# Rows of eight tokens for the selected blocks: sixteen gathers in place of thirty-two, in groups tied to neighbouring results, and slabs of x tied in the same way

## The chip, the cores and the metric

One core of a Trainium2 chip runs the whole program, in fp32. The metric is the device time of one execution in microseconds (us); lower is better. TensorE is called PE below, VectorE DVE, ScalarE ACT, GpSimd POOL, and SyncE SP, whose queue issues most of the transfers.

## What is computed

Two layers of a decoder are applied to a prompt of 1024 tokens and to 8 samples of one new token each. Layer 0 has an attention with three branches (compressed, selected blocks, window) beside a convolution module, then an output projection and a feed-forward part. The change touches the selected branch of the samples: each sample and each of its two key/value heads picks 16 of 65 blocks of 64 tokens, and attends to their keys and values, which lie in a paged cache of HBM.

```
def select_blocks(p_cmp, t_pos, ns):
    ...
    score = jnp.where(forced, BIG, jnp.where(valid, score, -BIG))
    _, idx = lax.top_k(score, min(N_SELECT, ns))
    return idx

def nsa_sample(q, kv_c, kv_s, kv_w, gates, ck, li, pool_c, pool_s, win_buf, page_table):
    ...
    idx = select_blocks(p_c, t_pos, ns)
    key_pos = idx[..., None] * SEL_BLOCK + jnp.arange(SEL_BLOCK)
    ...
    phys = page_table[bi, jnp.clip(key_pos // PAGE_SIZE, 0, n_pages - 1)]
    from_pool = pool_s[li, phys, key_pos % PAGE_SIZE, :, gi]
    ...
    o_s = selected_attention(q, t_pos, idx, sel)
```

After the attention `x_prompt` and `x_sample` get the output projection added: `xp = xp + concat([a_out, c_out]) @ w_out_a`. That sum is the x of the slabs below.

## The kernel before

The program is one stream of instructions for each engine. The Tile framework sets the order on each engine with a simulated schedule, so the order follows the order of the Python code, its priorities and the simulated times. The prompt's work is the foreground. The samples' work is a chain of Python generators started with `back=True`; `tick` (L85) advances a planned clock by the foreground's estimated time and takes the next piece of the chain when it is due, at lowered priority (`LAG`). A generator's `yield` is its planned time until the next piece; `WAIT[0]`, 35 us, stands between the issue of the key gathers and the first use of the keys.

The chain runs beside `prompt_attention` (L772) and `out_proj` (L1044) in this order: compressed tokens of the samples' caches (its gathers `pg<-ccmp` at L571), `dec_select` (L829), which ends in the row numbers `vidx` of the selected rows, `dec_gather_k` (L926), `dec_sel_scores` (L945), `dec_gather_v` (L985), `dec_values` (L1003).

**The gathers.** A row of the gathered tables `cslc_k` and `cslc_v` holds four tokens of one head: 256 elements, 1 KB. One sample and head needs 240 rows for its 15 old blocks, in two halves of 128 and 112 partitions. With 16 pairs of sample and head (four tiles of four pairs) that makes 32 indirect DMAs for the keys (L939) and 32 for the values (L996), issued by POOL in its order:

```
for h in range(2):
    m = P - 16 * h
    nc.gpsimd.indirect_dma_start(out=k[:m, n // 2, h, n % 2], out_offset=None, in_=i["cslc_k"],
                                 in_offset=bass.IndirectOffsetOnAxis(
                                     ap=self.vidx[:m, h, 4 * b2 + n:4 * b2 + n + 1], axis=0))
```

`dec_sel_scores` transposes the keys on PE (L955, 64 transposes), copies them to SBUF on ACT (L105, tile `ks`) and multiplies them by the queries (L967). `dec_values` multiplies the weights by the values (L1027).

**The prompt's attention** beside the key gathers: scores (L678, L679), softmax on ACT and DVE, transposes of the weights (L743), copies to `pt` by ACT (L105) and DVE (L117) in turn, products with the values (L762).

**The slabs of x.** `out_proj` splits its inputs z into two parts (`prep`, L1055), loads eight tiles of `w_out` (L123), and for each of eight output tiles m and each chunk of 344 columns runs 24 matmuls (three products for each of eight input tiles, L1112 to L1114) and adds the result to x on DVE (L1080). x lies in four slabs of two output tiles, 1032 KB each. The first is loaded at L1074, the others at L1083, in the code right after an add:

```
a = nc.vector.tensor_tensor(xs, xs, ps, op=ALU.add)
if c == 0 and m % 2 == 0 and m < 6:
    with self.tc.issue_after(a.ins):
        nc.sync.dma_start(x[m // 2 + 1], i["xt"][:, m + 2:m + 4])
```

`issue_after` orders the instruction in the schedule; it puts no wait for the add into the program.

Of the kernel before, what the change touches and what calls it, by code (L numbers as in the profile page):

```python
# [12 lines left out]
I32 = mybir.dt.int32  # L13
# [7 lines left out]
P = 128  # L21
D = 1024
TP = 1024
NS = 8
# [8 lines left out]
KY = 0.8  # L33
LAG = 100
DY = 0.6
TAPLAG = (1000, 2500)
WAIT = (35.0, 5.0)
# [3 lines left out]
class Net:  # L41
# [612 lines left out]
    def att_s1(self, it):  # L654
# [34 lines left out]
        self.att_scale(it, st, br)  # L689

# [111 lines left out]
    def dec_prep(self):  # L802
        nc, i = self.nc, self.i
        nd = i["c_dec"].shape[1]
        dw = self.u([P, 2 * T], name="dw")
        self.dwp = nd

        def d(m, n, dt=F32):
            a = self.dwp
            self.dwp += n  # L810
            t = dw[:m, a:a + n]
            return t if dt == F32 else t.bitcast(dt)
        self.d = d
        cst = self.cst = dw[:, 0:nd]
        nc.sync.dma_start(cst, i["c_dec"])
        self.eb, self.own = cst[:64, 16:24], cst[:64, 358:374]
# [12 lines left out]
    def dec_select(self):  # L829
        nc, d, cst, tb = self.nc, self.d, self.cst, self.tb  # L830
        hsum = cst[:64, 0:16]
        esel, iota62, addv = cst[:16, 24:280], cst[:16, 280:342], cst[:, 342:358]
# [46 lines left out]
        vp = self.ps(self.to(), [P, 2, 16])  # L879
        for h in range(2):  # L880
            nc.tensor.matmul(vp[:, h], esel[:, h * P:(h + 1) * P], pht, start=True, stop=True)
        self.vidx = self.small(P, 32, I32).rearrange("p (a b) -> p a b", a=2)
        nc.vector.scalar_tensor_tensor(self.vidx, vp, 32.0, addv[:, None, :].to_broadcast([P, 2, 16]),
                                       op0=ALU.mult, op1=ALU.add)
        yield DY * 2.0
        self.dec_gather_k()
# [42 lines left out]
    def dec_gather_k(self):  # L929

        nc, i = self.nc, self.i
        self.ksel = []
        self.dw2 = self.u([P, 2 * T], name="dw2")
        for b2 in range(4):
            k = self.u([P, 2, 2, 2, 256], name="ks")
            for n in range(4):
                for h in range(2):
                    m = P - 16 * h
                    nc.gpsimd.indirect_dma_start(out=k[:m, n // 2, h, n % 2], out_offset=None, in_=i["cslc_k"],  # L939
                                                 in_offset=bass.IndirectOffsetOnAxis(  # L940
                                                     ap=self.vidx[:m, h, 4 * b2 + n:4 * b2 + n + 1], axis=0))
            self.ksel.append(k)

    def dec_sel_scores(self):

        nc = self.nc
        yield WAIT[0]
        for b in range(NS):
            k = self.ksel[b // 2][:, b % 2]
            for h in range(2):  # L950
                m = P - 16 * h
                tp = self.ps(self.to(), [P, 512])
                kt = k[:, h].rearrange("p g c -> p (g c)")
                for e in range(4):
                    nc.tensor.transpose(tp[:, e * m:(e + 1) * m], kt[:m, e:512:4], self.ident[:m, :m])  # L955
                self.acopy(kt[:, :4 * m], tp[:, :4 * m])
                if h:
                    nc.vector.tensor_copy(kt[:, 448:449], self.knew[:, 0, b:b + 1])
                yield DY * 0.4
        dw = self.dw2  # L960
        p = dw[:64, 0:961]
        for h in range(2):
            n = 512 - 63 * h
            ps = self.ps(self.to(), [64, 512])
            for b in range(NS):
                kt = self.ksel[b // 2][:, b % 2, h].rearrange("p g c -> p (g c)")
                nc.tensor.matmul(ps[:, :n], self.qz[:, b], kt[:, :n], start=b == 0, stop=b == NS - 1)  # L967
                yield DY * 0.8
            self.acopy(p[:, 512 * h:512 * h + n], ps[:, :n])
# [4 lines left out]
        self.new_key(p, 960, 0)  # L974
        tp = self.ps(self.to(), [P, 4, 2, 64])
        for h in range(2):
            m = P - 16 * h
            for e in range(4):
                nc.tensor.transpose(tp[:m, e, h], p[:, 512 * h + e * m:512 * h + (e + 1) * m], self.ident[:64, :64])
        self.pst = dw[:, 1024:1536].rearrange("p (e h b) -> p e h b", e=4, h=2)  # L980
        self.acopy(self.pst[:, :, 0], tp[:, :, 0])
        self.acopy(self.pst[:112, :, 1], tp[:112, :, 1])
        yield WAIT[1]

    def dec_gather_v(self):  # L985
# [4 lines left out]
        for b2 in range(4):  # L990
            v = self.u([P, 4, 2, 256], name="vsel")
            for e in range(4):
                n = 4 * b2 + e
                for h in range(2):
                    m = P - 16 * h
                    nc.gpsimd.indirect_dma_start(out=v[:m, e, h], out_offset=None, in_=i["cslc_v"],  # L996
                                                 in_offset=bass.IndirectOffsetOnAxis(ap=self.vidx[:m, h, n:n + 1],
                                                                                     axis=0))
# [3 lines left out]
    def dec_values(self):  # L1002
# [3 lines left out]
        for hf in range(2):  # L1006
# [15 lines left out]
            for j in (2 * hf, 2 * hf + 1):  # L1022
                o = ov[:, 256 * (j % 2):256 * (j % 2) + 256].rearrange("p (n d) -> p n d", n=4)
                for h in range(2):
                    m = P - 16 * h
                    for e in range(4):
                        nc.tensor.matmul(o, self.pst[:m, e, h], self.vsel[j][:m, :, h, 64 * e:64 * e + 64],  # L1027
                                         start=False, stop=j % 2 == 1 and h == 1 and e == 3)
                        yield DY * 0.45
# [16 lines left out]
    def out_proj(self):  # L1046
# [21 lines left out]
        def part(chunks):  # L1068
            ws = [self.load_w(i["w_out"][0])]
            for m in range(8):  # L1070
# [4 lines left out]
                for c in chunks:  # L1075
# [396 lines left out]
def dec_consts():  # L1472
    c = np.zeros((P, 374), np.float32)
# [5 lines left out]
    for h in range(2):  # L1479
        c[:16, 24 + h * P:24 + (h + 1) * P] = bg[:, None] == (8 * h + p // 16)[None, :]  # L1480
    c[:16, 280:342] = np.arange(62)
    c[:, 342:358] = (bg % 2)[None, :] * 16 + (p % 16)[:, None]
    c[row, 358 + row // 4] = 1.0
# [3 lines left out]
def arrange(a):  # L1487
# [37 lines left out]
    r["cslc_k"] = cs[:, :, 0].reshape(-1, 16, 4, 2, 64).transpose(0, 3, 1, 4, 2).reshape(-1, 256)  # L1525
    r["cslc_v"] = cs[:, :, 1].transpose(0, 2, 1, 3).reshape(-1, 256)
# [51 lines left out]
```

## Time and profile before

| | |
|---|---|
| median of 3 runs | 2500.28 us (2498.76 to 2510.8) |
| the profiled execution | 2508.53 us |
| its span, first to last instruction | 2506.8 us |
| PE busy in the span | 2380.4 us (95%), 15040 matmuls |
| DVE, ACT, POOL busy | 53%, 30%, 8% |
| granted PE clock, mean of the span | 0.970 |

A span is the time from the first to the last instruction; a share is busy time over the span. In the windows of the section on rows, each engine's busy us stands with its count of instructions in brackets, then the granted PE clock as a fraction of full speed, the busy share of the 16 DMA engines, and GB/s. In a timeline a row gives start and duration in us, engine, line, operation, what it writes and reads, the count of merged instructions, and in square brackets the engine's idle time before it and what ended that.

### The profile page before, as it was taken

To read this page: it belongs to the slowest core of one execution; us is meant where nothing else is said; L and a number is where in the kernel's file an instruction comes from. 1 tells how busy PE (TensorE), PEld (TensorE's weight loads), DVE (VectorE), ACT (ScalarE), POOL (GpSimd) and SP (SyncE) were. 2 spreads that over 40 slices of the span, in tenths; PEclk is the share of its full clock that TensorE was granted. 3 is DMA by queue.
4 is the path that set the end of the run, shared out by engine and by line. 5 is a ranking of instruction groups with operands and counts; after the bars stand their busy time and mean duration, and the time that the engine had idled before them with its cause. 6 is when DMAs were issued, how large, how long until landed. Compare 5 with 4: busy or idle time off the path is not lost.

```text
span 2506.8 us, 36521 instructions
## 1 busy us (share of the span) xinstructions
PE 2380.4 (95%) x15040; PEld 2214.4 (88%) x15040; DVE 1324.6 (53%) x2261; ACT 745.4 (30%) x1415; POOL 210.2 (8%) x209
## 2 busy tenths in 40 slices
PE   8999889999876999999999999997999999999998
PEld 7999767677544799999999999986999999999997
DVE  7999565534531463444444444568544444444446
ACT  5113576655541252111111111134311111111102
POOL 0001313243224020000000000000000000000000
PEclk9999899999977999999999999998999999999999
DMA  5131324244116141311111111111211111111101
GB/s 176 35 119 60 120 78 142 84 128 120 40 51 221 59 127 51 118 50 50 52 34 51 51 51 51 42 34 49 71 44 41 51 41 44 51 51 51 51 9 68
DMA packets 79986, 176.77 MB, mean 71 GB/s; under 512 B 15468, under 2 KB 45932, under 8 KB 78316
## 3 DMA queue, kind: packets, MB, share of 16 engines
q1 hardware_dynamic: 70460, 149.68, 19.1%
q0 software_dynamic: 9216, 24.65, 3.3%
q8 instruction: 118, 1.93, 0.3%
q14 instruction: 48, 0.39, 0.0%
q10 hardware_dynamic: 144, 0.11, 0.0%
HBM read 160.51 MB, written 19.01 MB: 72 GB/s over the span
## 4 chain that ended last, share of the span: by engine, by line
PE 88%; DVE 4%; ACT 4%; issue 2%; another core or an unknown queue 1%; DMA 1%; POOL 0%; DVEq 0%; ACTq 0%; POOLq 0%; SPq 0%
PE ps L1114 21%; PE ps L1113 21%; PE ps L1112 21%; PE ps L584 5%; PE ps L743 3%; PE ps L136 3%; PE ps L134 3%; PE ps L135 3%; PE ps L762 2%; PE ps L678 1%; PE ps L679 1%; PE ps L1357 1%; PE ps L967 1%; PE ps L1027 1%
## 5 line engine op out<-in xcount | busy, mean ns | idle before, releaser
L1112 PE MATMUL ps<-hh,w 128*128 128x344 f32 x2112 | 678.5, 321 | 14.6 <-DVE sg L1209 13.9
L1113 PE MATMUL ps<-hl,w 128*128 128x344 f32 x2112 | 678.5, 321 | 0.2 <-DVE hl L1371 0.2
L1114 PE MATMUL ps<-hh,w 128*128 128x344 f32 x2112 | 678.4, 321 | 0.0
L1227 DVE TENSOR_TENSOR x<-x,ps 128x344 f32<-128x344 f32 x528 | 267.0, 512 | 288.1 <-PE ps L1114 286.2
L1112 PEld LDWEIGHTS ps<-hh,w 128*128 128x128 f32 x2112 | 398.9, 189 | 16.9 <-DVE sg L1209 14.8
L1113 PEld LDWEIGHTS ps<-hl,w 128*128 128x128 f32 x2112 | 398.8, 189 | 1.0 <-DVE hl L1371 0.4
L1114 PEld LDWEIGHTS ps<-hh,w 128*128 128x128 f32 x2112 | 398.7, 189 | 0.5
L105 ACT ACTIVATE w<-raw 128x1024 fp32r<-128x1024 f32 x170 | 177.7, 1057 | 708.0 <-PE ps L1114 674.8
L1112 PE MATMUL ps<-ah,w 128*128 128x344 f32 x1056 | 338.9, 321 | 0.7 <-ACT rt L1125 0.7
L1114 PE MATMUL ps<-ah,w 128*128 128x344 f32 x1056 | 338.4, 320 | 0.0
L1113 PE MATMUL ps<-al,w 128*128 128x344 f32 x1056 | 337.8, 320 | 0.0
L1209 DVE TENSOR_TENSOR sg<-ps,rs 128x688 f32<-128x688 f32 x132 | 115.2, 873 | 310.2 <-PE ps L1114 309.6
L109 DVE TENSOR_TENSOR w<-raw,w 128x1024 fp32r<-128x1024 f32 x170 | 211.2, 1243 | 90.9 <-ACT w L105 88.9
L1112 PEld LDWEIGHTS ps<-ah,w 128*128 128x128 f32 x1056 | 198.7, 188 | 1.5 <-ACT rt L1125 0.9
L1113 PEld LDWEIGHTS ps<-al,w 128*128 128x128 f32 x1056 | 198.4, 188 | 0.5
L1114 PEld LDWEIGHTS ps<-ah,w 128*128 128x128 f32 x1056 | 198.4, 188 | 0.0
L1210 ACT ACTIVATE sg<-sg 128x344 f32<-128x344 f32 x132 | 64.9, 492 | 376.6 <-DVE sg L1209 376.5
L571 POOL DMA_INDIRECT pg<-ccmp,aux x128 | 126.5, 989 | 471.4 <-PE ps L136 241.4
L134 PE MATMUL ps<-hh,w 128*128 128x344 f32 x456 | 150.2, 330 | 11.8 <-ACT w L105 9.9
L136 PE MATMUL ps<-hh,w 128*128 128x344 f32 x456 | 149.3, 329 | 4.9 <-DVE w L109 4.9
L135 PE MATMUL ps<-hl,w 128*128 128x344 f32 x456 | 148.7, 326 | 0.3 <-DVE hl L109 0.3
L392 DVE SCALAR_TENSOR_TENSOR y<-ext,vec,y 128x1011 f32<-128x1011 f32 (+28 forms) x120 | 147.5, 1271 | 0.5
(304 smaller groups left out, 2965.4 us busy)
## 6 DMA issues: line engine op xcount, KB each, us to landing
raw<-w_gate SPq DMA_DIRECT2D x44, 512.0 KB
raw<-w_up SPq DMA_DIRECT2D x44, 512.0 KB
raw<-w_down SPq DMA_DIRECT2D x44, 512.0 KB
pg<-ccmp SPq DMA_DIRECT2D x128, 128.0 KB
raw<-w_in SPq DMA_DIRECT2D x22, 512.0 KB
raw<-w_out SPq DMA_DIRECT2D x16, 512.0 KB
x<-xt SPq DMA_DIRECT2D x12, 344.0 KB
x<-xt SPq DMA_DIRECT2D x4, 1032.0 KB
```

What stands on the lines that cost most here:

```text
L105: return self.nc.scalar.activation(out, in_, AF.Copy, scale=scale)
L109: (eng or self.nc.vector).tensor_tensor(lo, src, hi.bitcast(F32), op=ALU.subtract)
L134: nc.tensor.matmul(ps, wh, xh[k], start=first and k == 0, stop=False)
L135: nc.tensor.matmul(ps, wh, xl[k], start=False, stop=False)
L136: nc.tensor.matmul(ps, wl, xh[k], start=False, stop=last and k == n - 1)
L392: nc.vector.scalar_tensor_tensor(y[:, z:TP], e[:, 0:TP - z], self.cw[:, j, k:k + 1], y[:, z:TP], op0=ALU.mult, op1=ALU.add)
L571: nc.gpsimd.indirect_dma_start(out=dst, out_offset=None, in_=i["ccmp"], in_offset=bass.IndirectOffsetOnAxis(ap=self.pidx[:, m:m + 1], axis=0))
L584: nc.tensor.matmul(ps[:, s], self.w1[:, s, k * P:(k + 1) * P], raw[:, :, s, k].rearrange("p a (g c) -> p g a c", g=2), start=k == 0, stop= ...
L1112: nc.tensor.matmul(ps, wh, xh[k], start=n == 0, stop=False)
L1113: nc.tensor.matmul(ps, wh, xl[k], start=False, stop=False)
L1114: nc.tensor.matmul(ps, wl, xh[k], start=False, stop=n == len(order) - 1)
L1227: nc.vector.tensor_tensor(xs, xs, ps, op=ALU.add)
```

## The change

- The tables hold rows of eight tokens (512 elements, 2 KB). The 240 rows of a sample and head become 120 on 120 partitions, so there are 16 gathers for the keys and 16 for the values, of the same bytes in all. The constants `c_dec` shrink from 374 to 246 columns, one small matmul of `dec_select` goes, and the transposes have 120 columns and partitions in place of 128 and 112.
- The gathers come in four groups of four, one group to a tile. Between groups the generator yields `GAP`, 6 us of the planned clock, and an ACT copy writes one element of the new tile, element 0 of partition 0, from `self.mark`. A mark is a slice of a recent result of the foreground: the softmax statistics `st` of an attention item, or the sum x of an add. Only the gather that writes over element 0 depends on that copy.
- `WAIT[0]` is 10 us in place of 35. The transposed keys go to other tiles than the ones they come from (an extra tile `kx`, then the tiles already read), and tile 3 is reused for the scores.
- Each later slab of x gets its first element written by an ACT copy of the add's result before its load. The load overwrites that element, so it waits for the copy and so for the add.

```diff
-WAIT = (35.0, 5.0)
+NSEL = 120
+WAIT = (10.0, 5.0)
+GAP = 6.0
...
+        self.mark = st[:1, 2, 0:1]
...
-        for h in range(2):
-            nc.tensor.matmul(vp[:, h], esel[:, h * P:(h + 1) * P], pht, start=True, stop=True)
+        nc.tensor.matmul(vp, esel, pht, start=True, stop=True)
...
-        self.dw2 = self.u([P, 2 * T], name="dw2")
+        self.kx = self.u([P, 2, 1024], name="kx")
         for b2 in range(4):
-            k = self.u([P, 2, 2, 2, 256], name="ks")
+            k = self.u([P, 2, 1024], name="ks")
+            if b2:
+                yield GAP
+                self.acopy(k[:1, 0, 0:1], self.mark)
             for n in range(4):
-                for h in range(2):
-                    m = P - 16 * h
-                    nc.gpsimd.indirect_dma_start(out=k[:m, n // 2, h, n % 2], ...
+                nc.gpsimd.indirect_dma_start(out=k[:NSEL, n // 2, 512 * (n % 2):512 * (n % 2) + 512], ...
...
-            v = self.u([P, 4, 2, 256], name="vsel")
+            v = self.u([P, 4, 512], name="vsel")
+            if b2:
+                yield GAP
+                self.acopy(v[:1, 0, 0:1], self.mark)
...
-                    a = nc.vector.tensor_tensor(xs, xs, ps, op=ALU.add)
+                    nc.vector.tensor_tensor(xs, xs, ps, op=ALU.add)
+                    self.mark = xs[:1, 0:1]
                     if c == 0 and m % 2 == 0 and m < 6:
-                        with self.tc.issue_after(a.ins):
-                            nc.sync.dma_start(x[m // 2 + 1], i["xt"][:, m + 2:m + 4])
+                        self.acopy(x[m // 2 + 1][:1, 0, 0:1], self.mark)
+                        nc.sync.dma_start(x[m // 2 + 1], i["xt"][:, m + 2:m + 4])
```

How the order on the engines moves, at three places. In these lists a row has the line, the operation, output and input tiles with their numbers, the shape, and the semaphores that it waits for; `DMASW` is the completion of an earlier gather, `Activation`, `DVE` and `PE` are results of those engines. The line numbers of the lists of the change are those of the changed file, where L941 is the key gather.

**POOL, the end of the key gathers.** `ks` is a tile of keys, `vsel` one of values, `sm` holds the row numbers. Before:

```order
L939 DMA ks_683_6641<-cslc_k,sm_1590 128x256 [waits DMASW4_49]
L939 DMA ks_683_6641<-cslc_k,sm_1590 112x256 [waits DMASW5_49]
L939 DMA ks_683_6641<-cslc_k,sm_1590 128x256 [waits DMASW6_49]
L939 DMA ks_683_6641<-cslc_k,sm_1590 112x256 [waits DMASW7_49]
L996 DMA vsel_871_7731<-cslc_v,sm_1590 128x256 [waits DMASW0_49,PE_49]
```

and with the change:

```order
L941 DMA ks_696_6708<-cslc_k,sm_1590 120x512 [waits DMASW7_49,Activation_49]
L941 DMA ks_696_6708<-cslc_k,sm_1590 120x512 [waits DMASW0_49]
L941 DMA ks_696_6708<-cslc_k,sm_1590 120x512 [waits DMASW1_49]
L941 DMA ks_713_6811<-cslc_k,sm_1590 120x512 [waits DMASW2_49]
L941 DMA ks_713_6811<-cslc_k,sm_1590 120x512 [waits DMASW3_49]
L941 DMA ks_713_6811<-cslc_k,sm_1590 120x512 [waits DMASW4_49]
L941 DMA ks_681_6618<-cslc_k,sm_1590 120x512 [waits DMASW5_49,Activation_49]
L941 DMA ks_696_6708<-cslc_k,sm_1590 120x512 [waits DMASW6_49,Activation_49]
L941 DMA ks_713_6811<-cslc_k,sm_1590 120x512 [waits DMASW7_49,Activation_49]
L996 DMA vsel_871_7716<-cslc_v,sm_1590 120x512 [waits DMASW0_49,PE_49]
```

The four of the first tile and three each of the others stand first, without a wait for a mark. The three that write element 0 of tiles 681, 696 and 713 are the last three of the sixteen. (The `Activation` wait of the first row shown is for a much older result, the last use of the slot.)

**ACT, the marks of the keys.** `p` and `st` are the softmax weights and statistics of the prompt's attention. Before:

```order
L105 ACTIVATE p_743_7012<-p_743_7012,st_745_7014 128x640 [waits DVE_49,Activation_49]
L105 ACTIVATE p_744_7013<-p_744_7013,st_745_7014 128x640 [waits Activation_49]
L688 ACTIVATE p_761_7126,st_763_7128<-ps_765_7137,st_763_7128 128x896 [waits DVE_49]
```

```order
L107 ACTIVATE p_743_6998<-p_743_6998,st_745_7000 128x640 [waits DVE_49,Activation_49]
L107 ACTIVATE p_744_6999<-p_744_6999,st_745_7000 128x640 [waits Activation_49]
L107 ACTIVATE ks_681_6618<-st_671_6562 1x1
L107 ACTIVATE ks_696_6708<-st_691_6675 1x1 [waits DMAHW2_49]
L107 ACTIVATE ks_713_6811<-st_709_6780 1x1
L690 ACTIVATE p_778_7219,st_780_7221<-ps_782_7232,st_780_7221 128x896 [waits DVE_49]
```

All three stand together, and read the statistics 671, 691 and 709 of items that come before 745, the one being scaled there.

**ACT and SP, the marks of the values and of x, in the output projection.** `x_854` to `x_857` are the four slabs, `vsel_872` to `vsel_879` the later tiles of values, `zh` a split input, `w` the leading part of a weight tile. ACT with the change (none of the 1x1 copies is there before):

```order
L107 ACTIVATE zh_849_7660<-z_865_7697 128x2x344 [waits DMAHW3_49]
L107 ACTIVATE x_855_7666<-x_854_7665 1x1 [waits DMAHW2_49,DVE_49]
L107 ACTIVATE vsel_872_7721<-x_854_7665 1x1
L107 ACTIVATE ks_696_6708<-ps_774_7198 128x480 [waits DMASW1_49,PE_49]
L107 ACTIVATE zh_846_7657<-z_907_8254 128x2x344 [waits DMAHW6_49]
L107 ACTIVATE zh_847_7658<-z_908_8258 128x2x344 [waits DMAHW1_49]
L107 ACTIVATE ks_713_6811<-ps_775_7205 64x480 [waits DMASW7_49,PE_49]
L107 ACTIVATE w_876_7780<-raw_875_7778 128x1024 [waits DMAHW4_49,PE_49,Activation_49]
L107 ACTIVATE vsel_874_7773<-x_854_7665 1x1 [waits SP_sequencer_49,DMAHW5_49,DVE_49,Activation_49]
```

SP with the change:

```order
L125 DMA raw_886_7913<-w_out 128x1024 [waits DMAHW0_49,DVE_49]
L1059 DMA z_908_8258<-cdram_2812 128x2x344 [waits DMAHW1_49,DVE_49]
L1082 DMA x_855_7666<-xt 128x2064 [waits DMAHW2_49,Activation_49]
L1061 DMA z_909_8262<-attd_2321 128x2x336 [waits DMAHW3_49,DVE_49]
L1061 DMA z_910_8267<-attd_2321 128x2x336 [waits DMAHW5_49,DMAHW6_49,DMAHW4_49,DVE_49]
L125 DMA raw_891_7992<-w_out 128x1024 [waits DVE_49]
L125 DMA raw_896_8071<-w_out 128x1024 [waits DMAHW7_49,DVE_49]
L1018 DMA vw_885_7909<-swin_v 128x4x512 [waits DMASW5_49,DMASW6_49,DMASW4_49,PE_49]
L1082 DMA x_856_7667<-xt 128x2064 [waits DMAHW0_49,Activation_49]
```

The second slab's load stands behind the first five weight tiles (886 is the fifth), as it did before, and now waits for ACT. The weights of the sixth and seventh tile (891, 896), which came behind all the slabs before, stand right behind it. On POOL the values' gathers stand as seven without a mark (tile 871, and three of 872), the one held by the first mark, three of 874, the held one, three of 879, the held one.

## Rows read from the trace of the kernel before

**Rows 1.** The page: busy times, and PE and its clock in 40 slices.

```profile
PE 2380.4 (95%) x15040; PEld 2214.4 (88%) x15040; DVE 1324.6 (53%) x2261; ACT 745.4 (30%) x1415; POOL 210.2 (8%) x209
...
PE   8999889999876999999999999997999999999998
...
PEclk9999899999977999999999999998999999999999
...
PE 88%; DVE 4%; ACT 4%; issue 2%; another core or an unknown queue 1%; DMA 1%; POOL 0%; DVEq 0%; ACTq 0%; POOLq 0%; SPq 0%
```

**Rows 2.** Windows between 562 and 804 us; columns as in the section on the profile.

```profile
562.00:600.00 38.00, 38.00 (x302) 31.20 (x301) 15.91 (x37) 18.70 (x49) 22.86 (x24) 1.00 0.58 174
665.00:676.50 11.50, 11.11 (x72) 6.87 (x70) 6.28 (x9) 5.56 (x12) 8.87 (x9) 1.00 0.34 97
676.50:705.00 28.50, 2.25 (x9) 0.90 (x9) 0.43 (x1) 3.05 (x4) 21.64 (x23) 0.57 0.33 99
705.00:718.00 13.00, 11.34 (x45) 7.51 (x45) 4.50 (x13) 5.06 (x16) 0.03 (x1) 0.50 0.04 11
757.00:778.00 21.00, 20.11 (x59) 9.09 (x60) 4.15 (x6) 3.29 (x6) 15.80 (x17) 0.87 0.90 299
778.00:798.50 20.50, 4.67 (x16) 3.41 (x15) 1.40 (x4) 1.85 (x3) 12.13 (x13) 0.62 0.72 248
798.50:804.00 5.50, 5.50 (x21) 5.01 (x21) 2.19 (x5) 0.21 (x1) 0.00 (x0) 0.55 0.22 64
```

**Rows 3.** Timeline of PE, from the last matmul before the first hole.

```profile
676.43 0.22 PE L683 MATMUL ps<-mb 128*128 128x128 bf16 x1
682.77 1.05 PE L743 MATMUL ps<-ident,p 128*56 128x128 f32 x4 [6.12 <-ACT pt L105]
683.76 1.12 PE L762 MATMUL ps<-pt,vs 128*64 128x256 f32 x4
705.32 0.37 PE L703 MATMUL ps<-mb 128*128 128x256 bf16 x1 [20.44 <-DVE pt L117]
```

**Rows 4.** Timelines of DVE and ACT in the first hole.

```profile
704.57 0.69 DVE L117 COPY pt<-ps 128x512 f32<-128x512 f32 x1 [28.46 <-remote]
...
710.26 0.59 ACT L105 ACTIVATE pt<-ps 56x512 f32<-56x512 f32 x1 [13.52 <-remote]
```

**Rows 5.** Timeline of POOL: key gathers one, two and last; value gathers four and last.

```profile
665.04 0.94 POOL L939 DMA_INDIRECT ks<-cslc_k,sm  x1 [65.78 <-DVE sm L883]
666.28 0.94 POOL L939 DMA_INDIRECT ks<-cslc_k,sm  x1 [0.30 <-issue]
...
704.10 0.93 POOL L939 DMA_INDIRECT ks<-cslc_k,sm  x1 [0.30 <-issue]
...
757.32 1.27 POOL L996 DMA_INDIRECT vsel<-cslc_v,sm  x1 [5.55 <-ACT ks L105]
...
792.87 0.92 POOL L996 DMA_INDIRECT vsel<-cslc_v,sm  x1 [0.30 <-issue]
```

**Rows 6.** Timeline of PE into and out of the second hole, output projection.

```profile
778.58 0.32 PE L1113 MATMUL ps<-zl,w 128*128 128x344 f32 x1
778.74 0.32 PE L1114 MATMUL ps<-zh,w 128*128 128x344 f32 x1
781.50 0.32 PE L1112 MATMUL ps<-zh,w 128*128 128x344 f32 x1 [2.45 <-issue]
783.64 0.45 PE L1113 MATMUL ps<-zl,w 128*128 128x344 f32 x1 [1.82 <-issue]
...
798.33 0.44 PE L1112 MATMUL ps<-zh,w 128*128 128x344 f32 x1 [0.25 <-issue]
```

**Rows 7.** Timeline of SP: loads of x slabs.

```profile
759.00 0.46 SPq L1074 DMA_DIRECT2D x<-xt  x1
...
773.70 0.69 SPq L1083 DMA_DIRECT2D x<-xt  x1
...
788.50 0.70 SPq L1083 DMA_DIRECT2D x<-xt  x1
```

**Rows 8.** Timeline of POOL: earlier gathers of the compressed caches, fourth and fifth of 24.

```profile
566.30 0.95 POOL L571 DMA_INDIRECT pg<-ccmp,aux  x1 [0.30 <-issue]
568.76 0.94 POOL L571 DMA_INDIRECT pg<-ccmp,aux  x1 [1.51 <-DMA pg<-ccmp,aux]
```

**Rows 9.** Timelines: a small ACT result, and the score matmuls on PE.

```profile
711.07 0.19 ACT L715 ACTIVATION_READ_ACCUMULATOR p<-ps,stc 128x1 f32 x1
...
757.21 9.67 PE L967 MATMUL ps<-ks,sm 128*64 128x512 f32 x16 [0.63 <-ACT ks L105]
767.56 6.24 PE L967 MATMUL ps<-ks,sm 128*64 128x449 f32 x16 [0.68 <-issue]
```

More of the change, by code (lines that the diff above doesn't have):

```diff
@@ L815, in dec_prep @@
         nc.sync.dma_start(cst, i["c_dec"])
-        self.eb, self.own = cst[:64, 16:24], cst[:64, 358:374]
+        self.eb, self.own = cst[:64, 16:24], cst[:64, 230:246]
         self.pnt = d(NS, P).rearrange("p (a b) -> p a b", a=2)
@@ L878, in dec_select @@
         nc.vector.tensor_copy(pht, pp)
-        vp = self.ps(self.to(), [P, 2, 16])
-        for h in range(2):
-            nc.tensor.matmul(vp[:, h], esel[:, h * P:(h + 1) * P], pht, start=True, stop=True)
-        self.vidx = self.small(P, 32, I32).rearrange("p (a b) -> p a b", a=2)
-        nc.vector.scalar_tensor_tensor(self.vidx, vp, 32.0, addv[:, None, :].to_broadcast([P, 2, 16]),
-                                       op0=ALU.mult, op1=ALU.add)
+        vp = self.ps(self.to(), [P, 16])
+        nc.tensor.matmul(vp, esel, pht, start=True, stop=True)
+        self.vidx = self.small(P, 16, I32)
+        nc.vector.scalar_tensor_tensor(self.vidx, vp, 16.0, addv, op0=ALU.mult, op1=ALU.add)
         yield DY * 2.0
-        self.dec_gather_k()
+        yield from self.dec_gather_k()
         nc.vector.tensor_scalar(p, p, self.gd[:, 0:1], None, op0=ALU.mult)
@@ L932, in dec_gather_k @@
         self.ksel = []
[L933 removed]
+        self.kx = self.u([P, 2, 1024], name="kx")
         for b2 in range(4):
[L935 removed]
+            k = self.u([P, 2, 1024], name="ks")
+            if b2:
+                yield GAP
+                self.acopy(k[:1, 0, 0:1], self.mark)
             for n in range(4):
[L937 to L941 removed]
+                nc.gpsimd.indirect_dma_start(out=k[:NSEL, n // 2, 512 * (n % 2):512 * (n % 2) + 512], out_offset=None, in_=i["cslc_k"],
+                                             in_offset=bass.IndirectOffsetOnAxis(
+                                                 ap=self.vidx[:NSEL, 4 * b2 + n:4 * b2 + n + 1], axis=0))
             self.ksel.append(k)
@@ L947, in dec_sel_scores @@
         yield WAIT[0]
+        kts = [t[:, s] for t in [self.kx] + self.ksel[:3] for s in range(2)]
         for b in range(NS):
@@ L973, in dec_sel_scores @@
         yield DY * 2.0
[L974 to L982, printed above, removed]
+        self.new_key(p, 8 * NSEL, 0)
+        tp = self.ps(self.to(), [P, 8, 64])
+        for e in range(8):
+            nc.tensor.transpose(tp[:NSEL, e], p[:, e * NSEL:(e + 1) * NSEL], self.ident[:64, :64])
+        self.pst = dw[:, 1024:1536].rearrange("p (e b) -> p e b", e=8)
+        self.acopy(self.pst[:NSEL], tp[:NSEL])
         yield WAIT[1]
@@ L990, in dec_gather_v @@
         for b2 in range(4):
-            v = self.u([P, 4, 2, 256], name="vsel")
+            v = self.u([P, 4, 512], name="vsel")
+            if b2:
+                yield GAP
+                self.acopy(v[:1, 0, 0:1], self.mark)
             for e in range(4):
                 n = 4 * b2 + e
[L994 to L998, printed above, removed]
+                nc.gpsimd.indirect_dma_start(out=v[:NSEL, e], out_offset=None, in_=i["cslc_v"],
+                                             in_offset=bass.IndirectOffsetOnAxis(ap=self.vidx[:NSEL, n:n + 1],
+                                                                                 axis=0))
             self.vsel.append(v)
@@ L1023, in dec_values @@
                 o = ov[:, 256 * (j % 2):256 * (j % 2) + 256].rearrange("p (n d) -> p n d", n=4)
[L1024 to L1029, printed above, removed]
+                for e in range(8):
+                    nc.tensor.matmul(o, self.pst[:NSEL, e], self.vsel[j][:NSEL, :, 64 * e:64 * e + 64],
+                                     start=False, stop=j % 2 == 1 and e == 7)
+                    yield DY * 0.45
             nc.vector.tensor_tensor(t[:, 512 * hf:512 * hf + 512].rearrange("p (n d) -> p n d", n=8),
@@ L1472, in dec_consts @@
 def dec_consts():
-    c = np.zeros((P, 374), np.float32)
+    c = np.zeros((P, 246), np.float32)
     p = np.arange(P)
@@ L1478, in dec_consts @@
     bg = np.arange(16)
[L1479 to L1483, printed above, removed]
+    c[:16, 24:152] = bg[:, None] == (p // 8)[None, :]
+    c[:16, 152:214] = np.arange(62)
+    c[:, 214:230] = (bg % 2)[None, :] * 8 + (p % 8)[:, None]
+    c[row, 230 + row // 4] = 1.0
     return c
```

29 lines of the change are left out of this document (14 added, 15 removed).

## The prediction

> **What bounds the kernel now.** I read the page first. PE is busy for 95% of the span and makes up 88% of the chain that ended last, so only time in which PE stands or runs slowly can be won; the slices show where that is: one dip in slices 11 and 12 (about 630 to 750 us) and another just behind, with the clock down in the same slices [rows 1]. Windows around the dip show two holes [rows 2]. In the first, from 676.5 to 705 us, PE works 2.25 of 28.5 us. It then comes back at a granted clock of 0.50, the lower of its two levels (1.2 of 2.4 GHz), until about 718. In the second, from 778 to 798.5 us, PE starts 16 matmuls in 20.5 us, and the clock is low until about 804. The rest of the kernel has nothing like it, and this change touches both places.
>
> The timeline of PE gives the first hole's ends: the last normal matmul starts at 676.43, eight more come at 683, and the next at 705.32, which is put down to a DVE copy [rows 3]. But that copy and the ACT copy after it had themselves waited 28.46 and 13.52 us for "remote", which is no engine's work in this profile [rows 4]. They read PE's transposes, recorded long before: the results of PE became visible late. What ran meanwhile was POOL: 32 key gathers, one every 1.25 us (0.94 and 0.30 between), the first at 665.04 and the last at 704.10 [rows 5]. The hole begins 11.4 us into that burst and ends 1.2 us after its last gather has started. The DMA engines were no bound there: share 0.33, 99 GB/s [rows 2].
>
> The second hole has the same neighbour. From 757.32 on 29 value gathers follow each other, the last at 792.87 [rows 5]; PE's matmuls, 0.16 us apart until 778.74, come 2 to 3 us apart without any named wait, and are back in step at 798.33 [rows 6]. This time the DMA engines are full as well (0.90 share and 299 GB/s, then 0.72): slabs of x of 1032 KB were issued at 759.00, 773.70 and 788.50, in the middle of the gathers [rows 7, 2]. The counter-example lies earlier: 24 gathers of as many bytes, in fours with pauses of 1.4 to 2.2 us (the fifth follows the fourth after 1.51), ran from 562 to 600 us at a DMA share of 0.58, and PE was busy in all 38.00 us at full clock [rows 8, 2]. So neither gathers nor 174 GB/s do harm by themselves. Long unbroken runs of gathers do, in both places.
>
> **What the holes cost.** First: 28.5 - 2.25 = 26.25 us idle; behind it 11.34 busy us at clock 0.50 hold 5.7 us of work, so 5.7 more: 32 us. Second: 16 matmuls at the 0.16 us of the rows ahead are 2.6 of 20.5 us, 17.9 lost; 21 matmuls in the next 5.5 us are 3.4, 2.1 lost: 20 us. The ceiling is 52 us [rows 2, 6].
>
> **The key gathers.** There are 16 in place of 32. A POOL time of 2 KB rows is not in the trace; between half of 0.94 us (half as many rows in all) and twice it, I take 0.94 and the 0.30, because a gather has 120 rows where it had 128 or 112, and the rows' number is what those agree in. The groups are hardly held: on POOL the four of the first tile and three of each other come first, and the three held ones last; the three marks stand on ACT where the key gathers begin, and copy statistics finished long before. So POOL runs 16 in a row, 16 x 1.25 = 20.0 us. If PE stops again 11.4 us after the first and resumes 1.2 us after the sixteenth starts (18.8), 8.6 us of the hole stay, and I keep the whole 5.7 for the clock: 14.3 left, 17.7 won. The bounds are 0 left (the second hole began 21.6 us after the start of its run, later than this burst lasts) and 32 left (if bytes, not gathers, count).
>
> **The value gathers and the slabs.** By POOL's order they come as 7, 4, 4 and 1, each held group behind an add of the output projection. Seven take 8.8 us, less than 11.4: no stall by the same measure. The later three slabs are asked for one pair of output tiles at a time. I take back the 17.9, and leave the 2.1 for what PE may wait when the first seven, the first slab and window values still meet. The bounds are 0 and 20.
>
> **What is added.** Nine 1x1 copies on ACT: the nearest row is a one-column result of 0.19 us [rows 9], so under 3 us on an engine that is 30% busy, hidden by its own idle time. What they hold counts more. On ACT a mark of x waits for an add, and behind it stand the key copies, splits of z and the weights of a later tile. The add needs PE's last product of that tile; the next weight split behind a mark is for a tile two further on, 1.5 x 48 x 0.16 = 11.5 us of PE work away, against some 3 us for a wait on DVE and a copy. On SP a held slab has in front five weight tiles and behind it the sixth and seventh. It is let go after the first add, and they are needed 4.5 x 48 x 0.16 = 35 us later by the same count. A slab itself is asked for one pair of tiles ahead, 96 x 0.16 = 15 us, plus 9.67 + 6.24 us of score matmuls for the first [rows 9]. At the 299 GB/s of the full stretch its 1.06 MB take 3.5 us alone, 7 with as much beside it. On PE the key transposes come earlier (`WAIT` 10 for 35): about 40 matmuls of attention stand between the row numbers and the first of them, 6 us at the 72 in 11.5 us of the window before the hole [rows 2], or twice that where one counts as two there; and the gather it needs was first in line. The held value gathers are read after all adds that hold them, by over 200 matmuls. All of these at 0. The smaller transposes and the matmul less are under 1 us, at 0 too.
>
> **Sum.** 17.7 + 17.9 = 35.6 us off the profiled 2508.5: 2472.9. That execution lies 8.2 us above the median of the runs shown, so against the median, 2500.3 - 35.6 = 2464.7, say **2465 us**.
>
> **A rule against it.** The first hole shows PE's results 28.46 us late with only gathers running [rows 4, 5]. The Trainium skill, page "SBUF — State Buffer", section "Who interferes with whom", says that a DMA never contends with a compute engine, and that PE and ACT never wait on anyone at the memory's ports. By it the gathers could not have held PE, and the sum would be 0. The trace does not fit it as far as the holes' ends follow the gathers' ends twice; but no row names the cause, so it stays a rival.
>
> **Rivals.**
> - *Neither hole is the gathers' doing*, and the time stays near 2500 (2488 to 2504). For: the low DMA share in the first hole, and "remote" as the only releaser. Against: both ends of both holes, and the clean 24 gathers. 0.15.
> - *Both holes go*: the burst of 16 is short enough or its half number of rows is what counts. 2500.3 - 52 = 2448. For: the late start of the second hole. Against: a 20 us burst is longer than the 11.4 us that it took in the same place. 0.20.
> - *Only one goes.* If bytes count in the first, its 32 us stay and 18 to 20 are won, 2481; if the second is made by transfers that only shift, 17.7 are won, 2483. 0.15.
> - *A ring of waits*, slower. PE's late result delays an add or a statistic, ACT's mark waits for it in order, POOL's held gather waits for the mark, and PE waits for that gather. Each turn would cost the 13.52 us that ACT waited [rows 4]: three marks among the keys and three among the values make 6 x 13.5 = 81 us in place of the 52: 29 more, about 2529. It decides if a mark stands behind a result of the hole and its gather is needed before the next add. For: POOL, ACT and SP all run in order. Against: the keys' marks read old results, and the held values are needed late. 0.06.
>
> **How the numbers follow.** My forecast (2455 to 2476, part of the first hole left) has 0.42, and 0.02 is left for cases between. Under 0.5%, 12.5 us, a measurement here can't tell a change from none: faster means below 2487.8, which the forecast, both holes gone and one gone give, 0.42 + 0.20 + 0.15 = 0.77. Same is 0.16, slower 0.07. The range runs from 2446 (both gone, less the 1.5 us between the two lower runs) to 2492, which leaves out most of "neither" and the ring.
>
> **What would show it.** POOL with 16 key gathers in some 20 us from about 665, PE's hole there about 9 us long and starting some 11 us in; value gathers in runs of 7, 4, 4 and 1; slabs loaded one add apart; PE near 20 of 20 us in every window after 760. The first step is wrong if PE stands as long as before, or not at all, in the key burst; the second if matmuls still come 2 us apart while the gathers are apart; the cost terms if ACT or SP rows show long waits for the add and PE then waits for weights.

## The result, and the profile after

The change makes the kernel faster: 2475.38 us median (2470.37 to 2479.45, 4 runs) against 2499.57 us for the kernel before, ratio 0.9888 with a 95% interval of 0.9866 to 0.9909, so 23 to 34 us. The forecast was 2465, a gain of 35.6. The direction and the range held; the gain was some 8 to 11 us smaller than the sum.

The profiled execution took 2474.33 us. Its page, busy times, then PE and its clock in 40 slices:

```profile
PE 2378.3 (96%) x15038; PEld 2207.5 (89%) x15038; DVE 1323.4 (54%) x2261; ACT 746.6 (30%) x1423; POOL 185.3 (7%) x177
...
PE   8999799999899899999999999988999999999998
...
PEclk9999899999999999999999999988999999999999
```

The deep dip of [rows 1] has become shallow. Windows around the key gathers, columns as in [rows 2]:

```profile
656.00:665.50 9.50, 9.50 (x66) 6.06 (x64) 5.33 (x12) 6.12 (x16) 7.03 (x8) 1.00 0.58 163
665.50:675.00 9.50, 3.84 (x22) 2.06 (x19) 1.30 (x2) 3.03 (x4) 7.37 (x8) 0.82 0.67 188
675.00:678.00 3.00, 0.00 (x0) 0.00 (x0) 0.41 (x1) 0.00 (x0) 1.34 (x2) 0.50 0.72 186
678.00:685.00 7.00, 6.67 (x29) 4.76 (x29) 3.91 (x12) 4.46 (x15) 0.00 (x0) 0.50 0.08 24
```

and the timelines of POOL (first and last key gather) and PE (the pieces of the hole):

```profile
656.34 0.99 POOL L941 DMA_INDIRECT ks<-cslc_k,sm  x1 [65.82 <-DVE sm L885]
...
675.67 0.98 POOL L941 DMA_INDIRECT ks<-cslc_k,sm  x1 [0.30 <-issue]
```

```profile
666.58 0.65 PE L956 MATMUL ps<-ident,ks 120*128 120x120 f32 x4
671.89 1.05 PE L746 MATMUL ps<-ident,p 128*56 128x128 f32 x4 [4.66 <-issue]
672.88 1.12 PE L765 MATMUL ps<-pt,vs 128*64 128x256 f32 x4
678.33 0.37 PE L706 MATMUL ps<-mb 128*128 128x256 bf16 x1 [4.33 <-issue]
```

Sixteen gathers run without a pause, 1.29 us apart, as the order of POOL said. PE stops 10.9 us after the first one started and is back after 22.0 us, idle for 4.66 + 4.33 = 9.0 us where [rows 3] had 6.12 + 20.44 = 26.6. The second hole of [rows 6] is gone; PE is busy for 95.96 of the 100 us from 700 to 800.

Where the time went is seen best from four landmarks in both traces: the first key gather, the last write of the prompt's attention, and the last add to x in the first and the second pass over `w_out`. The landmarks behind the first gather, before and after, on SP and DVE:

```profile
751.36 0.38 SPq L773 DMA_DIRECT2D attd<-aux  x1
...
888.64 0.51 DVE L1080 TENSOR_TENSOR x<-x,ps 128x344 f32<-128x344 f32 x1 [2.03 <-PE ps L1114]
...
922.22 0.51 DVE L1080 TENSOR_TENSOR x<-x,ps 128x344 f32<-128x344 f32 x1
```

```profile
723.06 0.38 SPq L776 DMA_DIRECT2D attd<-aux  x1
...
843.97 0.51 DVE L1078 TENSOR_TENSOR x<-x,ps 128x344 f32<-128x344 f32 x1 [0.93 <-PE ps L1113]
...
883.36 0.50 DVE L1078 TENSOR_TENSOR x<-x,ps 128x344 f32<-128x344 f32 x1
```

Durations between the landmarks in us (the first from the span's start, the last to its end), with two experiments of below:

| | to first key gather | key stage | first pass | second pass | rest | span |
|---|---|---|---|---|---|---|
| before | 665.0 | 86.3 | 137.3 | 33.6 | 1584.6 | 2506.8 |
| change | 656.3 | 66.7 | 120.9 | 39.4 | 1588.8 | 2472.2 |
| keys held by landings (k_held) | 660.2 | 56.8 | 116.5 | 36.5 | 1584.3 | 2454.3 |
| no planned time for the values (v_gap0) | 658.7 | 67.6 | 114.7 | 34.0 | 1583.0 | 2458.0 |

The key stage gained 19.6 us and the first pass 16.4. The second pass lost 5.8. The first column differs by 8.7 us, but in front of the first key gather the change only takes away one small matmul and some constants, and over all profiles of this study that time scatters between 656.3 and 670.0; the profiled execution of before was a long one besides (2508.53 where its median is 2499.57). The last column lies between 1582.5 and 1586.7 in the other profiles and at 1588.8 in the change's, so its 4.2 are not put down to the change.

### The profile page after: what moved, and what is told of

Same layout as the page of the kernel before. It is cut to its first block, busy times and chain, and to the rows that moved or that the text cites. A ratio compares the mean times of both kernels' runs of the same rounds, so it can differ in the third digit from the quotient of the medians.

```text
span 2472.2 us, 36476 instructions
## 1 busy us (share of the span) xinstructions
PE 2378.3 (96%) x15038; PEld 2207.5 (89%) x15038; DVE 1323.4 (54%) x2261; ACT 746.6 (30%) x1423; POOL 185.3 (7%) x177
## 4 chain that ended last, share of the span: by engine, by line
PE 89%; DVE 4%; ACT 4%; issue 1%; DMA 1%; POOL 0%; SPq 0%; DVEq 0%; ACTq 0%; POOLq 0%
PE ps L1111 21%; PE ps L1112 21%; PE ps L1113 21%; PE ps L586 5%; PE ps L765 3%; PE ps L746 3%; PE ps L138 2%; PE ps L136 2%; PE ps L137 2%; PE ps L680 2%; PE ps L681 1%; PE ps L1356 1%; DVE y L394 1%; PE ps L1025 1%; PE ps L968 1%
## 5 line engine op out<-in xcount | busy, mean ns | idle before, releaser
L1111 PEld LDWEIGHTS ps<-hh,w 128*128 128x128 f32 x2112 | 398.6, 189 | 17.2 <-DVE sg L1208 15.5
```

The source lines that it names most:

```text
L1111: nc.tensor.matmul(ps, wh, xh[k], start=n == 0, stop=False)
```

## The experiments

Twelve kernels ran, in three batches. The kernel before ran beside each and took 2502.5, 2504.6 and 2510.4 us there, so absolute times of different batches are some us apart. They are compared by their ratio to before, and "gain" is 2500 us times one minus that ratio, with its interval. The change gains 28 us (23 to 34) in this measure.

**What holds PE: the keys held by their own landings (k_held).** In the change's key gathers:

```diff
-                self.acopy(k[:1, 0, 0:1], self.mark)
+                q = [t.rearrange("p s (h c) -> p (s h) c", h=2)[:1, :, 0:1] for t in (k, self.ksel[-1])]
+                nc.gpsimd.tensor_copy(q[0], q[1])
```

> The key gathers are held by their own landings: in place of the ACT copy of a mark, a POOL copy takes one element of each of the four gathers of the tile before and writes it to the four places that the next four gathers overwrite, so POOL goes on only when the four have landed. All else as in the change. Gathers in long runs hold PE: four runs of four in some 28 us, the hole of 9.0 us idle and about 5.5 us of half clock beside the key gathers goes, 14 us less than the change (2475): about 2461. Rival, the bytes count (the same bytes move in nearly the same time): the hole stays, 2475. Rival, PE waits for the later keys at its transposes instead: idle of PE put down to DMA ks, 2470 or more.

2456.2 us, ratio 0.9813 (0.9795 to 0.9831), gain 47 (42 to 51). POOL's timeline, the fourth gather, the copy and the fifth:

```profile
664.06 0.98 POOL L942 DMA_INDIRECT ks<-cslc_k,sm  x1 [0.30 <-issue]
668.32 0.67 POOL L940 COPY ks<-ks 1x4 f32<-1x4 f32 x1 [3.28 <-DMA ks<-cslc_k,sm]
669.28 0.98 POOL L942 DMA_INDIRECT ks<-cslc_k,sm  x1 [0.29 <-POOL ks L940]
```

A pause of about 4 us after every four gathers, and the key stage falls from 66.7 to 56.8 us. PE's window from 660 to 680 us shows 19.79 busy at full clock while the gathers run:

```profile
660.00:680.00 20.00, 19.79 (x139) 12.39 (x139) 12.69 (x24) 14.05 (x33) 10.64 (x12) 1.00 0.42 109
680.00:700.00 20.00, 16.70 (x105) 10.00 (x106) 11.43 (x22) 11.98 (x23) 10.32 (x12) 0.96 0.54 151
```

The second row holds a rest: the fourth group of keys is followed at once by four of the values, eight in a run, and PE stops behind them (timeline of PE, k_held):

```profile
698.35 0.96 PE L957 MATMUL ps<-ident,ks 120*128 120x120 f32 x4 [2.78 <-issue]
```

The theory that long runs of gathers hold PE is borne out. The gain over the change, 19, is more than the 14 expected, but the key stage holds only 9.9 of it; the two passes behind came out 4.4 and 2.9 us shorter.

**Two runs of eight, and one of twelve (k_eights, k_twelve).** In k_eights the POOL copy stands before the ninth gather only; in k_twelve POOL clears the three later tiles after the fourth gather:

```diff
-                self.acopy(k[:1, 0, 0:1], self.mark)
+            if b2 >= 2:
+                q = [t.rearrange("p s (h c) -> p (s h) c", h=2)[:1, :, 0:1] for t in (k, self.ksel[1])]
+                nc.gpsimd.tensor_copy(q[0], q[1])
```

```diff
-                self.acopy(k[:1, 0, 0:1], self.mark)
+                nc.gpsimd.memset(k[:, :, 0:1024], 0.0)
```

> The change with the key gathers in two runs of eight: POOL goes on to the ninth when the fifth to eighth have landed; no marks for the keys. Values and slabs as in the change. What counts is the length of an unbroken run, with the hole starting 10 to 11 us in: eight take 8 x 1.29 = 10.3 us, so the hole is gone or under 2 us, 2460 to 2465. Rival, the gathers add up whatever the pause: 2472 to 2478.

> The change with the key gathers as a run of four, a pause in which POOL clears the three later tiles (the gathers write over all that is used), and a run of twelve. No marks for the keys. Length of a run: twelve take 15.5 us, so PE stops some 10 us in and is idle 4 to 6 us, with up to 5 us of low clock behind it: 2466 to 2471. Rival, only the total counts: 2475 or more. Rival, twelve are still harmless: 2461.

k_eights: 2467.2 us, ratio 0.9839 (0.982 to 0.9858), gain 40 (36 to 45). k_twelve: 2479.58 us, ratio 0.9877 (0.9857 to 0.9898), gain 31 (26 to 36). Both absolute times are some 6 to 8 us long (before took 2510.4 beside them); by the gains the first lies 12 above the change and the second 3, where 10 to 15 and 4 to 9 were expected. The key stages can be compared directly, since PE starts nearly the same work in each: 346 matmuls in that of before, 349 in the change's, 330 to 353 in the others. What sorts them is the longest unbroken run of gathers in the stage, and the values count in it where they follow the keys at once, as in k_held and in keys_only, which is described below (POOL's timeline of keys_only, the last key and the first of eight values):

```profile
699.29 0.98 POOL L942 DMA_INDIRECT ks<-cslc_k,sm  x1 [0.30 <-PE ps L681]
700.58 0.99 POOL L994 DMA_INDIRECT vsel<-cslc_v,sm  x1 [0.30 <-ACT kx L107]
```

| longest unbroken run | kernel | key stage, us |
|---|---|---|
| 32 | before | 86.3 |
| 16 | change, x_free, v_free, rows8, v_gap0 | 66.7, 64.4, 66.2, 66.8, 67.6 |
| 12 | k_twelve; keys_only (four keys and eight values) | 60.9; 59.5 |
| 8 | k_eights; k_held, both_held, both_held_x_free (four keys and four values) | 56.1; 56.8, 56.2, 56.4 |
| 4 | fours_1kb, the next experiment | 51.1 |

Runs of eight are not harmless: they cost some 5 us against runs of four, which leave PE at full clock, as these windows of k_eights and fours_1kb show:

```profile
660.00:680.00 20.00, 18.32 (x104) 11.67 (x101) 10.28 (x23) 10.70 (x27) 12.84 (x16) 0.79 0.54 152
```

```profile
660.00:680.00 20.00, 20.00 (x145) 13.40 (x143) 12.69 (x29) 14.40 (x35) 10.26 (x14) 1.00 0.24 69
```

Beyond the fourth, each gather of the longest run costs the stage about its whole slot: 51.1 + 4 x 1.29 = 56.3 for eight, 51.1 + 8 x 1.29 = 61.4 for twelve, 51.1 + 12 x 1.29 = 66.6 for sixteen, 51.1 + 28 x 1.25 = 86.1 for thirty-two. This is a fit to five lengths, with its base from one run. Of the two runs of eight in k_eights only the first leaves a hole. The waits put down to "remote" follow: 28.5 us the longest before, then 10.8, 5.2 and 4.4 (views of waits of the change, k_twelve and k_eights), and none in fours_1kb:

```profile
DVE pt L119 <- remote: 10.8, 1, 10.8
```

```profile
DVE pt L119 <- remote: 5.2, 1, 5.2
```

```profile
ACT pt L107 <- remote: 4.4, 1, 4.4
```

**Gathers of 1 KB, held in fours (fours_1kb).** The kernel before, with one addition for the keys, and the same for the values:

```diff
+                if n % 2 == 0 and (b2 or n):
+                    nc.gpsimd.tensor_copy(kg[:1, n // 2, :, 0:1], last)
+                last = kg[:1, n // 2, :, 0:1]
```

> The kernel before with its 32 and 32 gathers of 1 KB rows, and one thing added: after every four gathers POOL copies one element of each into the places that the next four overwrite, so it goes on when the four have landed. Slabs, waits and order otherwise as before. Long unbroken runs of gathers hold PE: both holes go although nothing of the rows or slabs changes, 2500 less 52, plus up to 10 us for keys that land too late (32 gathers in eight fours take some 66 us): 2448 to 2460. Rival, the bytes or the number of rows and slabs count: the holes stay, 2490 to 2500.

2467.17 us, ratio 0.9855 (0.9837 to 0.9874), gain 36 (32 to 41): most of the 52, if less than the 40 to 52 expected, without one byte, row or slab changed. No wait for "remote" is left from 640 to 720 us, and of PE's waits without a named cause, which made the second hole, 0.7 us are left from 700 to 900. The key stage runs from the first to the second of these rows, 51.1 us:

```profile
656.42 0.95 POOL L943 DMA_INDIRECT ks<-cslc_k,sm  x1 [65.79 <-DVE sm L883]
...
707.55 0.38 SPq L773 DMA_DIRECT2D attd<-aux  x1
```

The bytes and the number of rows are out as causes, of both holes. Most of what is missing are two new waits of PE, as the view of its waits shows, for keys and for window values that land late:

```profile
PE ps L1029 <- DMA vw<-swin_v: 5.6, 1, 5.6
PE ps L959 <- DMA ks<-cslc_k,sm: 5.6, 1, 5.6
```

**No key gathers at all (k_plain).** Sixteen plain loads on SP, of rows that are not the selected ones, take the place of the gathers:

```diff
-                nc.gpsimd.indirect_dma_start(out=k[:NSEL, n // 2, ...
+                r = NSEL * (4 * b2 + n)
+                nc.sync.dma_start(k[:NSEL, n // 2, 512 * (n % 2):512 * (n % 2) + 512], i["cslc_k"][r:r + NSEL])
```

> The change with the key gathers replaced by 16 plain loads of 120 rows of the same table on SP, each of the same bytes into the same places: the rows are not the selected ones, so the keys are others. Nothing else differs. POOL's gathers hold PE: the hole of 9.0 us idle and the half clock behind it go, 2475 - 14 = 2461. Rival, the bytes that reach the memory hold PE however they were asked for: the hole stays, 2475.

2464.49 us, ratio 0.9845 (0.983 to 0.986), gain 39 (35 to 43). PE is busy for 20.00 of the 20 us from 660 to 680 and no wait for "remote" is left before 715. But SP issued these loads between 468 and 639 us, ahead of the row numbers, so this run says that the hole needs the gathers, and not that bytes at their pace would be harmless. That is told by other rows: the hole of before had 99 GB/s, and 174 GB/s of gathers in fours did no harm [rows 2].

**Rows of eight alone (rows8), free slabs (x_free), free values (v_free).** rows8 has neither marks nor planned gaps, 35 us before the use of the keys and the slabs as before; x_free has only the edit below the dots, v_free only the one above them:

```diff
             v = self.u([P, 4, 512], name="vsel")
-            if b2:
-                yield GAP
-                self.acopy(v[:1, 0, 0:1], self.mark)
...
-                        self.acopy(x[m // 2 + 1][:1, 0, 0:1], self.mark)
-                        nc.sync.dma_start(x[m // 2 + 1], i["xt"][:, m + 2:m + 4])
+                        with self.tc.issue_after(a.ins):
+                            nc.sync.dma_start(x[m // 2 + 1], i["xt"][:, m + 2:m + 4])
```

> Rows of eight tokens alone: no marks, no planned 6 us, 35 us before the keys' use as before, slabs as before. The number of gathers in a run counts: keys 16 in a row as in the change, 14 us lost there in place of 32; values in runs of 10 to 14 beside early slabs, some 10 us lost in place of 20: 2499.5 - 28 + 0 = 2472 to 2480, so most of the change's gain. Rival, the holding apart did the work: 2490 or more. Rival, full queues: the second hole whole, 2482.

> The slabs of x are loaded as before the change (ordered behind the add, no wait on the chip); gathers as in the change. Gathers in long runs hold PE: no second hole, PE busy 95% or more between 700 and 800 us, time within 4 us of the change: 2471 to 2479. Rival, the second hole was made by full DMA queues (slabs on top of gathers): matmuls 2 to 3 us apart come back while the DMA share is near 1, some 18 us: 2493.

> The value gathers without marks and without the planned 6 us between groups; key gathers and slabs as in the change. They then stand on POOL as a run of up to ten and one of four or more behind each other. Gathers in long runs hold PE: if POOL runs 12 to 16 without a pause (15 to 20 us), a hole of 4 to 9 us with the low clock behind it comes in the output projection, 2479 to 2489, less what the earlier end of the samples' chain saves at the end of the first pass over w_out (PE idle there 6.5 us in the change). Rival, full queues: the slabs are still held, so no hole, 2469 to 2475.

rows8: 2464.55 us, ratio 0.9836 (0.9816 to 0.9856), gain 41 (36 to 46). x_free: 2474.08 us, ratio 0.9893 (0.9876 to 0.9911), gain 27 (22 to 31). v_free: 2461.5 us, ratio 0.9838 (0.9823 to 0.9853), gain 41 (37 to 44). The holding of the slabs does nothing that can be measured, and the second hole does not come back without it, though the queues are as full in x_free as they were in that hole:

```profile
740.00:760.00 20.00, 20.00 (x66) 9.59 (x65) 4.45 (x6) 4.74 (x7) 7.58 (x8) 0.93 0.98 295
```

PE is busy throughout, so full queues did not make the hole. rows8 and v_free came out under every time expected of them (2472 and 2469 at the least). In both, ten values follow each other beside the projection (in v_free from 722.52 to 735.21), and no wait for "remote" came of it: the price by length in the table above is that of the key stage alone. And the rows alone beat the change, clear of the intervals: what is added to them, the marks and planned gaps, costs 13 us. v_free puts that on the values.

**Planned time or marks (v_gap0).** Only the planned 6 us between groups of values go:

```diff
             if b2:
-                yield GAP
                 self.acopy(v[:1, 0, 0:1], self.mark)
```

> The change without the planned 6 us between the groups of values; their marks stay, as do keys and slabs. The planned time costs: 18 us of it put the samples' chain late, so that its matmuls with the values stand pair by pair between those of the projection and end where the first pass over w_out ends. Without it 2458 to 2465, as with the marks gone too (2461.5). Rival, the marks themselves cost (POOL and ACT standing on them): 2472 to 2478.

2459.88 us, ratio 0.9825 (0.9806 to 0.9843), gain 44 (39 to 49). The planned time it is. Two costs can be seen. In the change, PE's products with the values stand one pair at a time between those of the projection (timeline of PE, the change):

```profile
790.38 0.65 PE L1025 MATMUL ps<-vsel,ks 120*64 120x256 f32 x2
790.96 0.43 PE L1112 MATMUL ps<-zl,w 128*128 128x344 f32 x1
791.22 0.33 PE L1113 MATMUL ps<-zh,w 128*128 128x344 f32 x1
791.39 0.31 PE L1111 MATMUL ps<-zh,w 128*128 128x344 f32 x1
791.63 0.65 PE L1025 MATMUL ps<-vsel,ks 120*64 120x256 f32 x2
```

A pair and three products take 1.25 us, so the pair costs 1.25 - 3 x 0.16 = 0.77. In v_gap0 the sixteen pairs of the first half come in one piece, 7.07 us or 0.44 each:

```profile
785.90 7.07 PE L1024 MATMUL ps<-vsel,ks 120*64 120x256 f32 x32
```

With 21 of 32 pairs alone in the change that is 21 x 0.33 = 7 us, about the 6.2 by which the first pass is shorter in v_gap0. And the samples' chain ends where the second pass begins, so PE waits there for its results and for splits of weights that stand behind it (timeline of PE, the change):

```profile
839.87 0.42 PE L1111 MATMUL ps<-zh,w 128*128 128x344 f32 x1 [1.88 <-ACT sm L107]
...
845.08 0.42 PE L1111 MATMUL ps<-zh,w 128*128 128x344 f32 x1 [1.15 <-ACT w L107]
...
847.67 0.43 PE L1113 MATMUL ps<-zh,w 128*128 128x344 f32 x1 [2.01 <-DVE w L111]
```

These 5.0 us are most of the 5.4 by which the second pass is longer than in v_gap0. So the two passes show 11.6 of the 16 us between the two gains, 44 and 28; the rest is within their intervals.

**Putting it together (both_held, both_held_x_free, keys_only).** Keys and values held by landings, then with free slabs, then only the keys held and all else free, all three without planned time for the values. For the values of the first two:

```diff
             if b2:
-                yield GAP
-                self.acopy(v[:1, 0, 0:1], self.mark)
+                nc.gpsimd.tensor_copy(v[:1, :, 0:1], self.vsel[-1][:1, :, 0:1])
```

> Keys and values both held by the landing of the four before (POOL copies as in the run with held keys), no marks and no planned time for the values, slabs as in the change. Both theories together (long runs of gathers hold PE, and the planned time of the values costs 14 us): 2456 - 14 = 2442, between 2438 and 2448. Rival for the values, the pauses of POOL put them as late as the marks did: 2452 to 2460.

> Keys and values held by the landing of the four before, and the slabs of x loaded as before the change. In the run with both held and the slabs behind ACT's copies, a copy for a slab stood on ACT behind a copy of scores that waited 6.2 us for PE, the slab landed late and PE waited 5.2 us for an add. Held slabs cost that: 2450, between 2445 and 2454. Rival, free slabs fall on the gathers and bring part of the second hole back: 2457 or more.

> Only the keys are held, by the landing of the four before; values without marks and planned time, slabs as before the change; rows of eight. The rows alone gave 2464.5 with 14 us lost beside the keys: 2450, between 2446 and 2455. Rival, values unheld cost a hole of their own beside the slabs, since the values now come right behind the keys: 2456 or more.

both_held: 2457.28 us, ratio 0.9821 (0.9797 to 0.9845), gain 45 (39 to 51). both_held_x_free: 2460.8 us, ratio 0.9811 (0.9794 to 0.9829), gain 47 (43 to 52). keys_only: 2464.32 us, ratio 0.9815 (0.9798 to 0.9833), gain 46 (42 to 51). both_held misses the 58 of its expectation; the other two hold the 50 of theirs within their intervals, but none of the three can be told from k_held, which has the planned time still. The gains don't add. One thing that takes their place is a wait of PE in the first pass, in all three (views of PE's waits of both_held, both_held_x_free and keys_only):

```profile
PE ps L1111 <- DVE x L1078: 5.2, 1, 5.2
```

```profile
PE ps L1110 <- DVE x L1078: 4.2, 1, 4.2
```

```profile
PE ps L1108 <- DVE x L1076: 4.4, 1, 4.4
```

I had put it down to held slabs, and free slabs did not take it away. In both_held_x_free the add that PE waits for stands on DVE behind a reduction of the samples' scores, before which DVE idles for 15.5 us until ACT has copied them, and the second slab reaches SP's queue only at 764.92, late by order and not by a hold: it stands behind a load of window values that waits for the score matmuls. These begin 30 us behind the projection's first product there, and 15 us behind it in the change. An order without that wait was not tried.

## Why the prediction was right, and where it was not

**The first hole** was read rightly. 8.6 us of idle PE were to stay, 9.0 did; the key stage gained 19.6 where 17.7 were forecast. That POOL would run sixteen without a pause, because a mark of an old result holds nothing and only one gather of a group is tied to it, is what the trace shows. The closeness of 8.6 and 9.0 is luck in part: PE came back 2.7 us after the sixteenth gather's start and not 1.2, and worked for 2 us in between. A hole that begins some 11 us in and ends with the run was near enough for sixteen, but by it a run of eight, 10.3 us long, would be free, and it cost 5: PE stood for 1.7 us from 10.5 us after the start of the first run in k_eights, and at half clock behind that.

**The second hole** is gone as forecast, and for the reason given first, the run of gathers: it stayed away with free slabs (x_free), and it went in fours_1kb with nothing changed but the runs. The values came in runs of 4, 3, 4, 1, 3 and 1, where 7, 4, 4 and 1 were forecast. The first pass gained 16.4 of the 17.9, although it now carries 7 us for single pairs.

**"All of these at 0" failed.** Of what the change adds I priced the copies, the waits of ACT and SP on marks and the earlier transposes, and these did cost nothing that can be seen in the change. What was left out of the list is the planned 6 us between groups. I had read it as a hold on gathers; it is a delay of the chain behind it, and that moves the samples' matmuls on PE. By v_gap0 against the change it cost 16 us (44 less 28; the ends of the intervals allow 5 to 26), of which the passes show 11.6. The single pairs stand in the order of PE's instructions, which is fixed before anything runs.

**The sum against the median** was made from an execution that had lost 8.7 us in front of the first key gather. The holes' sizes did not depend on that, and subtracting their gain from the median was right; with the missing term the sum would have been 35.6 - 16 = 20, under the 23 to 34 measured. The two gather terms were a little small: 17.7 against the 19.6 of the key stage, and 17.9 against the 22.6 that the first pass gained in v_gap0.

**The rule against it** (the Trainium skill, page "SBUF — State Buffer", section "Who interferes with whom") would have given no gain, as the prediction read it. The trace does not agree with that reading: the gain came, and fours_1kb has it from the runs of gathers alone. The rule speaks of the memory's ports, and the runs do not show by which path a long run of POOL's gathers keeps PE's results back; no row names it. So the rule itself is neither borne out nor refuted here. Of the rivals, "neither hole" is out, "only one goes" too. The ring of waits did not form: the held values were needed long after.

## What to carry to other kernels

Where PE's results are waited for beside gathers, keep POOL's unbroken runs to four, counting gathers of the next stage that follow at once, and let the next group start on the landing of the last, by a copy on POOL itself. Longer rows shorten the runs: a gather of 2 KB rows took POOL 1.29 us where one of 1 KB rows took 1.25. A tie to "some recent result" holds nothing unless that result is late, so read in the order which result it is. Planned time in a background chain is not a pause of one queue: it moves everything behind it, and one has to look where that work then falls on the busiest engine.

## What was not expected of the hardware

In the key stage, each gather beyond the fourth of the longest unbroken run cost about its own 1.25 to 1.29 us, for runs of 8, 12, 16 and 32; with runs of four nothing of the kind was left. Lengths between four and eight were not tried, nor whether the pause or the landing in it is what matters. And a pair of plain fp32 matmuls placed alone between the projection's fp32r ones took 0.77 us of PE where it took 0.44 in a row of its kind.
